# GpSimd's scoring work queued behind the first candidates, in a decoder trunk with product-key experts

## The chip, the cores and the metric

The kernel runs on one core of a Trainium2 chip. Its time is the device time of one execution in microseconds; the number that counts is the median of the runs. The core has five engines with their own instruction queues: TensorE (PE, with its weight loads as PEld), VectorE (DVE), ScalarE (ACT), GpSimd (POOL) and SyncE (SP, which here only issues DMAs). Each queue is worked off in order. An instruction waits at the head of its queue until what it needs has been signalled, and all behind it wait too.

## The reference

A batch of one sequence of 512 tokens of 1024 features goes through two layers. Layer 0 mixes along the sequence with a gated linear recurrence, layer 1 with multi-head latent attention. Each mixer is preceded by an RMSNorm whose shift, scale and gate come from a conditioning vector, and each is followed by the same channel mixer, which is the larger part of the work:

```python
def peer(h, w_q, sub_keys, u_tab, v_tab):
    q = (h @ w_q).reshape(B, S, PEER_HEADS, 2, PEER_HALF)
    s = jnp.einsum('bshpd,hpnd->bshpn', q, sub_keys)
    v1, i1 = lax.top_k(s[..., 0, :], 16); v2, i2 = lax.top_k(s[..., 1, :], 16)
    cand = v1[..., :, None] + v2[..., None, :]          # 256 sums per head
    cv, ci = lax.top_k(cand.reshape(..., 256), 16)      # best 16 pairs
    idx = e1 * 128 + e2                                 # one expert of 16384
    g = softmax(cv)
    act = gelu(einsum('bcd,bchkd->bchk', h, u_tab[idx]))
    out = einsum('bchk,bchkd->bcd', g * act, v_tab[idx])
```

The modulation vectors are `silu(c) @ ada_w + ada_b`: 112 columns of 128 values, each the sum over a row of 1024 products ("ada" below).

## The kernel before, in words

Tokens are four blocks of 128; features lie on partitions as eight chunks `k`. Products that need float32 precision are made of three matmuls: each operand is split into a high part (ACT copies it into the matmul's format, L179, `whi`) and a low part (source minus high part, L180, `wlo`, on an engine that the caller names), and `mm3` (L216 to L218) adds low times high, high times low and high times high. A weight or expert tile takes a DMA into `raw` (four buffers), one ACT instruction and one subtraction.

Each layer ends in `peer(l)`. Three of the four token blocks are computed densely: for each of 128 expert tiles, `u_part` splits the tile of `u` and multiplies it with the activations of 384 tokens (24 matmuls of 128x384), ACT applies the gelu, and later the tile of `v` is multiplied with the gated result. The fourth block (number 3, `nd`) gathers the rows of its own experts by indirect DMA on GpSimd's queue and reduces them on DVE (`gather_steps`, L1479 to L1488, named `grow` and `gdot`). The stages are:

1. The head. The last products of the mixer (`wo`) come out in two halves of 256 tokens. For each half, DVE adds the residual (L383), ACT squares it (L287), and the squares are summed in `nacc`: three additions on GpSimd (chunks 1 to 3) and three on DVE (chunks 4 to 6), L288 in `half_sq`. PE sums `nacc` over the partitions (L297, outputs `wo` or `st`), ACT and DVE make the reciprocal root, PE turns it into a row, ACT copies it (L310). Then for each chunk DVE makes `xn` (L1091), ACT the high part of `h` (L1093), DVE the low part (L1094), and PE multiplies three tiles of the query weights with it as soon as a chunk is there (`pq`, L216 to L218).
2. Scoring, four groups of two heads. A group multiplies four tiles of query weights (`pq`, 96 matmuls of 128x512), scores the keys (`sc`, L1200), and DVE takes the top 16 for each of the four token blocks (L933 to L937). GpSimd adds the candidates (`cand`, two instructions for each block: L944 and L947), DVE takes the best pairs (L956 to L960). In the same stretch each group does `UPQ` = 3 expert tiles, and `adas_pool` makes 6 ada columns in layer 0 or 2 in layer 1. A column there is a load on SP's queue (two buffers), a multiplication on GpSimd (L168), a sum on ACT (L169); a column is closed by a small addition on GpSimd (L174). In this stretch all splits of weights and expert tiles after the first three `pq` tiles have their subtraction on GpSimd.
3. Decoding, on DVE, of block 3 first (its indices start the gathers) and then of block 0. `UDEC` expert tiles are written ahead of it.
4. Gates: for each 16 tokens of the three dense blocks, DVE makes two pairs of one-hot tiles (`oo` L1041, `pr` L1043), PE multiplies them (`wps`, 32 matmuls), ACT copies them out (L1052), and expert tiles go on in between.
5. The rest: `v` tiles (`acc`) with the remaining gathers.

The order on each engine is made when the program is built: a scheduler simulates the engines and takes what is ready first, by the order in the code. `tc.issue_after(ins)` is a constraint on it: what the block traces on the engine of `ins` is queued behind `ins`. It adds no wait on a semaphore, and it does not bind the other engines. `self.hold` does the same for the first splits against the last steps of the head on ACT and DVE.

Lines to know: `half_sq` L270 to L289, `adas_pool` L161 to L175, `wtile` L184 to L199, `candidates` L939 to L949, the scoring loop L1182 to L1211, `UDEC` at L47 and its use at L1216.

Of the kernel before, what the change touches and what calls it, by code (L numbers as in the profile page):

```python
# [16 lines left out]
OP = mybir.AluOpType  # L17
# [4 lines left out]
P = 128  # L22
D = 1024
KC = D // P
# [19 lines left out]
OWN = KC * T // ND  # L44
LEAD = OWN + RING - 3 + SPILL
UPQ = (3, 3, 3, 3)
UDEC = 13  # L47
UEND = 7
QUIET = 4
EARLY = 74  # L50
# [33 lines left out]
class Trunk:  # L84
# [854 lines left out]
    def candidates(self, pool, v, h0, n):  # L939
        nc = self.nc  # L940
        v4 = v.rearrange("p (h s) k -> p h s k", s=2)[:, h0:h0 + n]
        cand = pool.tile([P, n, NCAND], F32, name="cand", bufs=3)
        ca = cand[:, :, 0:64].rearrange("p h (i j) -> p h i j", j=16)
        nc.gpsimd.tensor_tensor(ca, v4[:, :, 0, 0:4].unsqueeze(3).to_broadcast([P, n, 4, 16]),  # L944
                                v4[:, :, 1, 0:16].unsqueeze(2).to_broadcast([P, n, 4, 16]), op=OP.add)
        cb = cand[:, :, 64:112].rearrange("p h (i j) -> p h i j", j=4)
        nc.gpsimd.tensor_tensor(cb, v4[:, :, 0, 4:16].unsqueeze(3).to_broadcast([P, n, 12, 4]),  # L947
                                v4[:, :, 1, 0:4].unsqueeze(2).to_broadcast([P, n, 12, 4]), op=OP.add)
        return cand  # L949

    def best_pairs(self, pool, cand, cv, ci, h0, n):
# [105 lines left out]
    def peer(self, l):  # L1057
        nc, io, tc = self.nc, self.io, self.tc
        nd = NB - 1
        with ExitStack() as st:  # L1060
# [6 lines left out]
            h = []  # L1067
# [54 lines left out]
            def ring(t):  # L1122
                held = (t - OWN) % RING < RING - 3
                return acts.tile([P, ND], F32, name="gact" if held else "gsp", bufs=RING - 3 if held else 3)
# [3 lines left out]
            def u_part(after=None, eng=None):  # L1128
                t = state["u"]
                state["u"] = t + 1  # L1130
                out = self.bank("u", True)
                hi, lo = self.wtile(io["uT"][l][t], KC, eng=eng or nc.vector)
                with tc.issue_after(after) if after is not None else ExitStack():
                    for k, (bh, bl) in enumerate(h):
                        self.mm3(out[:, :ND], (hi[:, k, :], lo[:, k, :]), (bh[:, :ND], bl[:, :ND]), k == 0, k == KC - 1)
                if t < OWN:
                    gact[t] = self.x.rearrange("p k t -> p (k t)")[:, t * ND:t * ND + ND]
                elif LEAD - SPILL <= t < LEAD:
                    g = acts.tile([P, ND], F32, name="gsp", bufs=3)
                    nc.scalar.activation(g, out[:, :ND], AF.Gelu)  # L1140
                    nc.scalar.dma_start(self.gscr[l, t - (LEAD - SPILL)], g)
                    return
                else:
                    gact[t] = ring(t)
                nc.scalar.activation(gact[t], out[:, :ND], AF.Gelu)
# [13 lines left out]
            def decodes(bs):  # L1159
                for b in bs:  # L1160
                    res = []
                    for _ in self.decode(dpool, cvs[b], cis[b], iu[b], res):
                        yield
                    if b == nd:
                        gsel.append(self.gather_index(gpool, l, *res))
                    else:
                        prep[b] = self.gate_prep(pool, *res)

            with tc.tile_pool(name=f"pq{l}", bufs=1) as pool:
                waiting = []  # L1170

                def settle(keep):
                    nonlocal gsteps
                    while len(waiting) > keep:
                        b, grp, cand = waiting.pop(0)
                        self.best_pairs(pool, cand, cvs[b], cis[b], 2 * grp, 2)
                        if grp == 3 and b == nd:
                            for _ in decodes((nd,)):
                                pass
                            gsteps = self.gather_steps(gpool, l, *gsel[0], hn)  # L1180

                for grp in range(4):  # L1182
                    keys = pool.tile([P, 4, P], F32, name="keys", bufs=2)
                    nc.scalar.dma_start(keys, io["keysT"][l][:, 4 * grp:4 * grp + 4, :])
                    outs = []
                    wq = l * 16 + 4 * grp
                    if grp == 0:
                        outs = pq0
                    qs = []
                    for m in range(4):  # L1190
                        if m >= len(outs):
                            outs.append(self.bank("pq"))
                            self.lin(outs[m], self.wtile(io["w_pq"][wq + m], KC, eng=nc.gpsimd), h)
                        q = pool.tile([P, T], F32, name="pq_s", bufs=5)
                        nc.scalar.activation(q, outs[m], AF.Copy)
                        qs.append(q)
                    for b in (nd, *range(nd)):
                        sc = self.bank("sc")
                        for m in range(4):
                            nc.tensor.matmul(sc[:, m * P:m * P + P], qs[m][:, b * P:b * P + P], keys[:, m, :],  # L1200
                                             start=True, stop=True)
                        for m in range(4):
                            last = self.topk_half(pool, sc[:, m * P:m * P + P], vs[b][:, 4 * grp + m, :],
                                                  iu[b][:, 4 * grp + m, :])
                        waiting.append((b, grp, self.candidates(pool, vs[b], 2 * grp, 2)))
                        settle(1)
                    self.hold = ()
                    self.adas_pool(6 if l == 0 else 2, pool)
                    for _ in range(UPQ[grp]):
                        u_part(eng=nc.gpsimd)  # L1210
                settle(0)  # L1211
            with tc.tile_pool(name=f"gate{l}", bufs=1) as pool:
                nsg = P // TG
                steps = decodes(range(nd))
                for i in range(UDEC):
                    u_part()  # L1216
# [5 lines left out]
                for i in range(nt):  # L1222
# [3 lines left out]
                    w, p = self.gate_group(pool, l, i // nsg, i % nsg, *prep[i // nsg])  # L1226
# [13 lines left out]
            grp, vls, vdma = {}, [], []  # L1240
# [110 lines left out]
            outs = [hpool.tile([P, D], F32, name=f"onat{b}", tag=f"h{b}") for b in range(nd)] + [next(gsteps)]  # L1351
# [232 lines left out]
```

## Time and profile before

| | us |
|---|---|
| median of 3 runs | 2978.91 |
| lowest and highest of these | 2976.91, 2980.32 |
| the profiled execution, its own time | 2977.65 |
| its span, first to last instruction | 2975.9 |
| PE busy | 2879.1 (97%) |
| DVE busy | 2500.0 (84%) |
| POOL busy | 1115.1 (37%) |

The profile's rows give start, duration, engine, line, operation, output and inputs; a bracket tells the idle time of the engine ahead of the instruction and what ended it. In a table of groups a row has the count, the busy time in us and the mean in ns. In the table of waits a row reads: engine, its instruction, what it waited for, us in total, how often, the longest. Matmuls overlap, so the time that one costs is the step from its start to the next one's, which is shorter than the duration in its row. PEclk is the granted clock of TensorE as a share of full speed.

### The profile page before, as it was taken

The page shows a single profiled execution, that of the slowest core. Times are in us where ns is not written, and L with a number is a line of the kernel's source. Part 1 is how long each engine was busy: PE and PEld are TensorE (multiplying, and loading weights), DVE is VectorE, ACT ScalarE, POOL GpSimd, SP SyncE. Part 2 cuts the span into 40 slices and gives each one's busy share as a digit, 9 for nine tenths or more (in the row PEclk, how much of TensorE's full clock was granted, in tenths as well). Part 3 has the DMA queues.
Part 4 walks back from the last instruction along what each step waited for, and adds up shares of the span by engine and source line. Part 5 has one row for each costly group of instructions (what it writes and reads, how often), then busy time and mean ns, then how long its engine had stood idle before and what let it go on. Part 6 is the DMA issues. An engine that isn't in the chain of part 4 may idle for free.

```text
span 2975.9 us, 43994 instructions
## 1 busy us (share of the span) xinstructions
PE 2879.1 (97%) x15680; PEld 2570.0 (86%) x15680; DVE 2500.0 (84%) x4709; ACT 1423.6 (48%) x2103; POOL 1115.1 (37%) x873
## 2 busy tenths in 40 slices
PE   7979998999999999999999989989999999999998
PEld 5679998999888889998878789989998888899997
DVE  8988799998888878879878877899985777788888
ACT  4755355665433333333576752456664333333333
POOL 4038514432222234535334455235331111244442
PEclk9989999999999999999999989999999999999999
DMA  8546349998999999999323333379999899999996
GB/s 317 186 156 198 115 158 345 360 370 325 338 361 360 361 320 356 320 346 326 107 85 130 123 138 103 114 276 346 371 355 315 300 336 323 309 329 353 347 337 220
DMA packets 296219, 813.71 MB, mean 273 GB/s; under 512 B 33152, under 2 KB 130560, under 8 KB 289600
## 3 DMA queue, kind: packets, MB, share of 16 engines
q1 hardware_dynamic: 188928, 439.41, 42.9%
q0 software_dynamic: 78912, 287.34, 27.0%
q10 hardware_dynamic: 28160, 84.14, 7.3%
q8 instruction: 124, 2.03, 0.3%
q14 instruction: 95, 0.78, 0.1%
HBM read 727.44 MB, written 83.36 MB: 272 GB/s over the span
## 4 chain that ended last, share of the span: by engine, by line
PE 86%; DVE 6%; ACT 3%; DMA 2%; issue 2%; POOL 1%; SPq 0%; ACTq 0%; DVEq 0%; POOLq 0%
PE acc L217 12%; PE acc L218 12%; PE acc L216 12%; PE u L216 12%; PE u L218 11%; PE u L217 11%; PE pq L217 2%; PE pq L218 2%; PE pq L216 2%; PE wps L1049 1%; PE wps L208 1%; PE sc L1200 1%; DVE wlo L180 1%; ACT whi L179 1%; DVE ada_junk L153 1%
## 5 line engine op out<-in xcount | busy, mean ns | idle before, releaser
L216 PE MATMUL u<-h,wlo 128*128 128x384 f32 x2048 | 692.3, 338 | 10.7 <-ACT gsp L1140 10.4
L218 PE MATMUL u<-h,whi 128*128 128x384 f32 x2048 | 689.3, 337 | 0.0
L217 PE MATMUL u<-h,whi 128*128 128x384 f32 x2048 | 687.8, 336 | 0.0
L1479 POOL DMA_INDIRECT grow<-in_u_dram,idx x256 | 340.5, 1330 | 714.2 <-DVE gdot L1483 449.7
L218 PE MATMUL acc<-vh,ah 128*128 128x512 f32 x1512 | 589.4, 390 | 0.0
L217 PE MATMUL acc<-vl,ah 128*128 128x512 f32 x1512 | 589.1, 390 | 0.0
L1479 POOL DMA_INDIRECT grow<-in_v_dram,idx x256 | 375.1, 1465 | 564.8 <-DVE gacc L1488 381.9
L216 PE MATMUL acc<-vh,al 128*128 128x512 f32 x1512 | 549.0, 389 | 1.1 <-ACT vh L179 1.1
L179 ACT ACTIVATE whi<-raw 128x1024 fp32r<-128x1024 f32 (+2 forms) x362 | 352.8, 976 | 176.0 <-PE u L218 67.1
L180 DVE TENSOR_TENSOR vl<-vraw,vh 128x1024 fp32r<-128x1024 f32 x252 | 308.6, 1225 | 122.7 <-ACT vh L179 121.5
L216 PEld LDWEIGHTS u<-h,wlo 128*128 128x128 f32 x2048 | 386.1, 189 | 16.3 <-ACT gsp L1140 13.3
L217 PEld LDWEIGHTS u<-h,whi 128*128 128x128 f32 x2048 | 385.9, 188 | 2.8
L218 PEld LDWEIGHTS u<-h,whi 128*128 128x128 f32 x2048 | 385.6, 188 | 0.0
L180 DVE TENSOR_TENSOR wlo<-raw,whi 128x1024 fp32r<-128x1024 f32 (+1 forms) x263 | 322.1, 1225 | 75.2 <-ACT whi L179 74.6
L218 PEld LDWEIGHTS acc<-vh,ah 128*128 128x128 f32 x1512 | 283.7, 188 | 59.2
L216 PEld LDWEIGHTS acc<-vh,al 128*128 128x128 f32 x1512 | 283.7, 188 | 58.4 <-ACT vh L179 1.5
L217 PEld LDWEIGHTS acc<-vl,ah 128*128 128x128 f32 x1512 | 283.8, 188 | 57.4
L1488 DVE SCALAR_TENSOR_TENSOR gacc<-grow,gdot,gacc 128x1024 f32<-128x1024 f32 x254 | 324.9, 1279 | 7.9 <-DMA grow<-in_v_dram,idx 6.8
L1483 DVE CUSTOM_DVE_ANT_0 grow<-grow,hn 128x1024 f32<-128x1024 f32 x256 | 308.5, 1218 | 13.8 <-DMA grow<-in_u_dram,idx 13.5
L179 ACT ACTIVATE ah<-gact 128x384 fp32r<-128x384 f32 x204 | 106.8, 523 | 425.5 <-PE acc L218 327.5
L179 ACT ACTIVATE vh<-vraw 128x1024 fp32r<-128x1024 f32 x252 | 264.2, 1048 | 57.8 <-issue 45.0
L1052 ACT ACTIVATE stg<-wps 128x512 f32<-128x512 f32 x192 | 188.8, 1113 | 58.2 <-PE wps L208 58.1
(421 smaller groups left out, 4595.9 us busy)
## 6 DMA issues: line engine op xcount, KB each, us to landing
raw<-in_uT_dram SPq DMA_DIRECT2D x256, 512.0 KB, 6.0
vraw<-in_v_dram SPq DMA_DIRECT2D x256, 512.0 KB, 6.2
wscr<-stg ACTq DMA_DIRECT2D x48, 1024.0 KB, 7.3
wt<-wscr SPq DMA_DIRECT2D x42, 1024.0 KB, 10.5
ada_raw<-in_adaw_dram SPq DMA_DIRECT2D x76, 512.0 KB, 4.3
gscr<-gsp ACTq DMA_DIRECT2D x132, 192.0 KB, 6.1
gact<-gscr SPq DMA_DIRECT2D x108, 192.0 KB, 6.4
ada_raw<-in_adaw_dram POOLq DMA_DIRECT2D x36, 512.0 KB, 6.2
```

The lines of the kernel that those rows point to most:

```text
L153: nc.vector.tensor_tensor_reduce(junk, raw, self.csil, op0=OP.mult, op1=OP.add, scale=1.0, scalar=b, accum_out=col)
L179: last = nc.scalar.activation(hi, src, AF.Copy)
L180: lo = (eng or nc.vector).tensor_tensor(lo, src, hi.bitcast(F32), op=OP.subtract)
L208: return pe.add_instruction(mybir.InstMatmult(name=self.nc.get_next_instruction_name(), start_tensor_calc=start, stop_tensor_calc=stop, ld ...
L216: nc.tensor.matmul(out, al, bh, start=first, stop=False, **kw)
L217: nc.tensor.matmul(out, ah, bl, start=False, stop=False, **kw)
L218: last = nc.tensor.matmul(out, ah, bh, start=False, stop=last, **kw)
L1049: lead = nc.tensor.matmul(out, w, pr[:, 0, a + t], start=True, stop=False).ins
L1052: nc.scalar.activation(stg[:, :, c:c + 4].rearrange("p e t -> p t e"), wps.rearrange("p (t e) -> p t e", t=4), AF.Copy, scale=1.0 / GSCALE)
L1479: nc.gpsimd.indirect_dma_start(out=row, out_offset=None, in_=tabs[s], in_offset=bass.IndirectOffsetOnAxis(ap=idx[:, k:k + 1], axis=0))
L1483: nc.vector.tensor_tensor_reduce(row, row, hn, op0=OP.mult, op1=OP.add, scale=1.0, scalar=0.0, accum_out=col)
L1488: nc.vector.scalar_tensor_tensor(acc, row, col, acc, op0=OP.mult, op1=OP.add)
```

## The change

Three edits. The second instruction of the first group's first candidates (those of block 3) becomes a mark, `first`. Ada columns, and from the second group on the splits of weight tiles, are queued behind that mark on GpSimd; the expert tiles are too. In the first group, the subtractions of the one weight tile and the three expert tiles go to DVE instead of GpSimd. And `UDEC` goes from 13 to 15.

```diff
-UDEC = 13
+UDEC = 15
...
     def candidates(self, pool, v, h0, n):
...
-        nc.gpsimd.tensor_tensor(cb, ...)
+        self.last_cand = nc.gpsimd.tensor_tensor(cb, ...).ins
...
-                waiting = []
+                waiting, first = [], None
...
                         if m >= len(outs):
                             outs.append(self.bank("pq"))
-                            self.lin(outs[m], self.wtile(io["w_pq"][wq + m], KC, eng=nc.gpsimd), h)
+                            with tc.issue_after(first) if first is not None else ExitStack():
+                                w = self.wtile(io["w_pq"][wq + m], KC, eng=nc.gpsimd if grp else nc.vector)
+                            self.lin(outs[m], w, h)
...
                         waiting.append((b, grp, self.candidates(pool, vs[b], 2 * grp, 2)))
+                        first = first or self.last_cand
                         settle(1)
                     self.hold = ()
-                    self.adas_pool(6 if l == 0 else 2, pool)
-                    for _ in range(UPQ[grp]):
-                        u_part(eng=nc.gpsimd)
+                    with tc.issue_after(first):
+                        self.adas_pool(6 if l == 0 else 2, pool)
+                        for _ in range(UPQ[grp]):
+                            u_part(eng=nc.gpsimd if grp else nc.vector)
```

From the scoring loop on, line numbers of the changed kernel are 1 to 4 higher (L1195 becomes L1197, L1483 becomes L1487).

The order of the queues shows what this moves. First GpSimd's queue in layer 0, from the additions of the head on; `nacc` is the sum of squares, `ada_raw` an ada column. Before:

```order
L288 TENSOR_TENSOR nacc_1459<-nacc_1459,sq_1469 128x256
L168 TENSOR_TENSOR ada_raw_2148<-ada_raw_2148,csil_66 128x1024
L288 TENSOR_TENSOR nacc_1459<-nacc_1459,sq_1479 128x256
L168 TENSOR_TENSOR ada_raw_2152<-ada_raw_2152,csil_66 128x1024
L288 TENSOR_TENSOR nacc_1459<-nacc_1459,sq_1489 128x256
L168 TENSOR_TENSOR ada_raw_2156<-ada_raw_2156,csil_66 128x1024
L288 TENSOR_TENSOR nacc_1459<-nacc_1459,sq_1545 128x256
L168 TENSOR_TENSOR ada_raw_2160<-ada_raw_2160,csil_66 128x1024
L288 TENSOR_TENSOR nacc_1459<-nacc_1459,sq_1555 128x256
L288 TENSOR_TENSOR nacc_1459<-nacc_1459,sq_1565 128x256
L168 TENSOR_TENSOR ada_raw_2164<-ada_raw_2164,csil_66 128x1024
L168 TENSOR_TENSOR ada_raw_2168<-ada_raw_2168,csil_66 128x1024
```

The same place in the changed kernel, where `cand_2013` are the first candidates (`v3` is block 3), `wlo_2274` is the first split of the second group, and `cand_2045` are the candidates of block 0:

```order
L288 TENSOR_TENSOR nacc_1459<-nacc_1459,sq_1469 128x256
L288 TENSOR_TENSOR nacc_1459<-nacc_1459,sq_1479 128x256
L288 TENSOR_TENSOR nacc_1459<-nacc_1459,sq_1489 128x256
L288 TENSOR_TENSOR nacc_1459<-nacc_1459,sq_1545 128x256
L288 TENSOR_TENSOR nacc_1459<-nacc_1459,sq_1555 128x256
L288 TENSOR_TENSOR nacc_1459<-nacc_1459,sq_1565 128x256
L947 TENSOR_TENSOR cand_2013<-v3_1924 128x2x48
L168 TENSOR_TENSOR ada_raw_2148<-ada_raw_2148,csil_66 128x1024
L168 TENSOR_TENSOR ada_raw_2152<-ada_raw_2152,csil_66 128x1024
L944 TENSOR_TENSOR cand_2013<-v3_1924 128x2x64
L180 TENSOR_TENSOR wlo_2274<-raw_2272,whi_2273 128x1024
L947 TENSOR_TENSOR cand_2045<-v0_1921 128x2x48
```

The six additions now stand together, with nothing between them and the first candidates. Before, thirteen ada multiplications and five splits stood between the first addition and the first candidates in layer 0, and eight and five in layer 1; now none do. Of the five splits, four are on DVE and one is behind the candidates.

Second, DVE's queue in layer 0 at chunks 3 to 7 of the head's second half (`xn` L1091 and `h` L1094; `h4_1722` is chunk 4), up to the first MAX of the scoring. Before:

```order
L1094 SCALAR_TENSOR_TENSOR h3_1705<-xn_1827,mod_91,h3_1705 128x256
L1091 SCALAR_TENSOR_TENSOR xn_1861<-x_68,gs_f0_1628,nacc_1459 128x256
L1094 SCALAR_TENSOR_TENSOR h4_1722<-xn_1845,mod_91,h4_1722 128x256
L1091 SCALAR_TENSOR_TENSOR xn_1877<-x_68,gs_f0_1628,nacc_1459 128x256
L1094 SCALAR_TENSOR_TENSOR h5_1736<-xn_1861,mod_91,h5_1736 128x256
L1091 SCALAR_TENSOR_TENSOR xn_1893<-x_68,gs_f0_1628,nacc_1459 128x256
L1094 SCALAR_TENSOR_TENSOR h6_1750<-xn_1877,mod_91,h6_1750 128x256
L1094 SCALAR_TENSOR_TENSOR h7_1764<-xn_1893,mod_91,h7_1764 128x256
```

And in the changed kernel, with the splits that came from GpSimd (`wlo_1954` is the fourth `pq` tile, the other three are the expert tiles of the first group):

```order
L1094 SCALAR_TENSOR_TENSOR h3_1705<-xn_1827,mod_91,h3_1705 128x256
L1091 SCALAR_TENSOR_TENSOR xn_1861<-x_68,gs_f0_1628,nacc_1459 128x256
L180 TENSOR_TENSOR wlo_1954<-raw_1952,whi_1953 128x1024
L180 TENSOR_TENSOR wlo_2176<-raw_2174,whi_2175 128x1024
L1094 SCALAR_TENSOR_TENSOR h4_1722<-xn_1845,mod_91,h4_1722 128x256
L1091 SCALAR_TENSOR_TENSOR xn_1877<-x_68,gs_f0_1628,nacc_1459 128x256
L1094 SCALAR_TENSOR_TENSOR h5_1736<-xn_1861,mod_91,h5_1736 128x256
L1091 SCALAR_TENSOR_TENSOR xn_1893<-x_68,gs_f0_1628,nacc_1459 128x256
L1094 SCALAR_TENSOR_TENSOR h6_1750<-xn_1877,mod_91,h6_1750 128x256
L1094 SCALAR_TENSOR_TENSOR h7_1764<-xn_1893,mod_91,h7_1764 128x256
L180 TENSOR_TENSOR wlo_2208<-raw_2206,whi_2207 128x1024
L180 TENSOR_TENSOR wlo_2240<-raw_2238,whi_2239 128x1024
```

Two splits now stand ahead of chunk 4, and two behind chunk 7, ahead of the first MAX.

Third, DVE's queue in layer 0 at the second group of gates: `pr` is what PE's `wps` waits for; `grow` with `gdot` is one gathered row block, which waits for its indirect DMA (`grow_4462` and `grow_4496` are the sixth, `grow_4465` and `grow_4499` the seventh). Before:

```order
L1483 ISA grow_4462,gdot_4284<-grow_4462,hn_1627 128x1024
L1483 ISA gdot_4284 128x1
L1043 TENSOR_TENSOR pr_4399<-oo_4398,gp_4143 128x2048
L1483 ISA grow_4465,gdot_4284<-grow_4465,hn_1627 128x1024
L1483 ISA gdot_4284 128x1
L180 TENSOR_TENSOR wlo_4645<-raw_4643,whi_4644 128x1024
L1043 TENSOR_TENSOR pr_4423<-oo_4422,gp_4143 128x2048
```

And in the changed kernel:

```order
L1487 ISA grow_4496,gdot_4352<-grow_4496,hn_1627 128x1024
L1487 ISA gdot_4352 128x1
L1487 ISA grow_4499,gdot_4352<-grow_4499,hn_1627 128x1024
L1487 ISA gdot_4352 128x1
L1043 TENSOR_TENSOR pr_4433<-oo_4432,gp_4209 128x2048
L180 TENSOR_TENSOR wlo_4573<-raw_4571,whi_4572 128x1024
L1043 TENSOR_TENSOR pr_4457<-oo_4456,gp_4209 128x2048
```

The seventh block stood behind the third `pr` and ahead of the fourth, and is now ahead of both. The number of splits that DVE does ahead of the first `pr` is 19 in both. On PE, between the scoring and the first `wps` stand 508 matmuls of `u` instead of 502, and between the first 32 `wps` and the next ones, which wait for the third `pr`, 66 matmuls of `u` instead of 48.

More of the change, by code (lines that the diff above doesn't have):

```diff
@@ L946, in candidates @@
         cb = cand[:, :, 64:112].rearrange("p h (i j) -> p h i j", j=4)
-        nc.gpsimd.tensor_tensor(cb, v4[:, :, 0, 4:16].unsqueeze(3).to_broadcast([P, n, 12, 4]),
-                                v4[:, :, 1, 0:4].unsqueeze(2).to_broadcast([P, n, 12, 4]), op=OP.add)
+        self.last_cand = nc.gpsimd.tensor_tensor(cb, v4[:, :, 0, 4:16].unsqueeze(3).to_broadcast([P, n, 12, 4]),
+                                v4[:, :, 1, 0:4].unsqueeze(2).to_broadcast([P, n, 12, 4]), op=OP.add).ins
         return cand
```

## The prediction

> **What bounds the kernel now.** I read the page first, then PE's waits by stage, then the windows, and the timelines of the two heads.
>
> ```profile
> span 2975.9 us, 43994 instructions
> PE 2879.1 (97%) x15680; PEld 2570.0 (86%) x15680; DVE 2500.0 (84%) x4709; ACT 1423.6 (48%) x2103; POOL 1115.1 (37%) x873
> ```
>
> PE is the bound: it idles 2975.9 − 2879.1 = 96.8 us of the whole span, so a change that takes no work off PE can only win idle time and time at a low clock. The change touches the two heads and what follows them. PE's waits there, first in layer 0 (178 to 240 us):
>
> ```profile
> PE wo L297 <- DVE nacc L288: 6.5, 1, 6.5
> PE pq L217 <- DVE h L1094: 5.9, 4, 2.5
> PE pq L216 <- ACT h L1093: 4.9, 1, 4.9
> ```
>
> In layer 1 (1700 to 1765 us):
>
> ```profile
> PE st L297 <- DVE nacc L288: 5.3, 1, 5.3
> PE pq L217 <- DVE h L1094: 5.3, 4, 2.6
> ```
>
> At the start of the gates in layer 0:
>
> ```profile
> PE wps L1049 <- DVE pr L1043: 8.1, 2, 5.5
> ```
>
> The windows give the same four places with the granted clock (busy us of PE, PEld, DVE, ACT, POOL, then PEclk, DMA share, GB/s):
>
> ```profile
> 181.80:239.70 57.90, 40.50 (x236) 38.31 (x236) 35.96 (x47) 31.73 (x67) 35.48 (x20) 0.76 0.47 166
> 1710.50:1761.50 51.00, 40.14 (x232) 37.33 (x232) 38.92 (x47) 29.49 (x62) 30.21 (x19) 0.80 0.40 145
> 451.00:471.00 20.00, 11.94 (x75) 11.54 (x74) 16.98 (x26) 7.62 (x9) 8.49 (x6) 0.74 0.98 367
> 1973.00:1993.00 20.00, 12.11 (x76) 11.71 (x75) 17.15 (x26) 7.34 (x9) 8.90 (x7) 0.74 0.99 376
> ```
>
> Layer 0's head idles 57.90 − 40.50 = 17.4 us, and what is busy runs at 0.76: at most 40.50 × 0.24 = 9.7 us more. Layer 1's idles 10.9 us and loses at most 40.14 × 0.20 = 8.0 us. The timeline of layer 0's head shows the clock in the steps between matmuls:
>
> ```profile
> 203.28 0.58 PE L217 MATMUL pq<-h,whi 128*128 128x256 f32 x1 [2.49 <-DVE h L1094]
> 211.34 0.28 PE L216 MATMUL pq<-h,xlo 128*128 128x256 f32 x1
> 211.46 0.28 PE L217 MATMUL pq<-h,xhi 128*128 128x256 f32 x1
> 218.27 0.58 PE L217 MATMUL pq<-h,whi 128*128 128x256 f32 x1 [1.57 <-DVE h L1094]
> 218.65 0.41 PE L218 MATMUL pq<-h,whi 128*128 128x256 f32 x1
> 218.86 0.41 PE L216 MATMUL pq<-h,xlo 128*128 128x256 f32 x1
> ```
>
> Behind a wait the step is 0.21 us (218.65 to 218.86), later 0.12 (211.34 to 211.46). From 203.28 to 211.34 PE did 31 products and eight small sums in 8.06 us, worth about 4.6 at the quick step (31 × 0.12, and the sums by half): 3.5 us lost in this stretch, and a second one begins at 218.27. I count 7 us in each head: 17.4 + 7 = 24.4 us lost in layer 0 and 10.9 + 7 = 17.9 us in layer 1. The gate starts lose 8.1 and 20.00 − 12.11 = 7.9 us of waiting, and 11.94 × 0.26 = 3.1 us each of clock.
>
> **The heads, what goes.** The timeline of the sums in layer 0:
>
> ```profile
> 178.73 0.74 POOL L288 TENSOR_TENSOR nacc<-nacc,sq 128x256 f32<-128x256 f32 x1 [11.64 <-ACT sq L287]
> 180.77 2.37 POOL L168 TENSOR_TENSOR ada_raw<-ada_raw,csil 128x1024 f32<-128x1024 f32 x1 [1.30 <-DMA ada_raw<-in_adaw_dram]
> 181.89 0.48 DVE L383 SCALAR_TENSOR_TENSOR x<-wo,mod,x 128x256 f32<-128x256 f32 x1 [0.17 <-PE wo L218]
> 186.84 1.48 DVE L288 TENSOR_TENSOR nacc<-nacc,sq 128x256 f32<-128x256 f32 x3 [4.47 <-POOL nacc L288]
> 188.38 1.01 PE L297 MATMUL wo<-ones,nacc 128*128 128x1 f32 x4 [6.53 <-DVE nacc L288]
> ```
>
> An ada multiplication of 2.37 us stands behind an addition of 0.74 us, and by the order of the queue another ahead of the third addition; DVE then waits 4.47 us and PE 6.53. PE came at 188.38 − 6.53 = 181.85. Without the multiplications GpSimd ends its three additions by 178.73 + 3 × 0.74 = 181.0, if the squares are there; DVE's three, at 0.49 each, can follow its residual of 181.89 or stand ahead of it, so they end at about 183.4 and PE waits **1.5 us** (0 to 2). In layer 1 GpSimd's additions have no ada ahead of them either; there I take **0** (0 to 1.5).
>
> Second, DVE's own chunk work is slower whenever GpSimd works:
>
> ```profile
> 222.05 4.74 POOL L180 TENSOR_TENSOR wlo<-raw,whi 128x1024 fp32r<-128x1024 f32 x2 [4.52 <-ACT whi L179]
> 224.40 2.67 DVE L1094 SCALAR_TENSOR_TENSOR h<-xn,mod,h 128x256 fp32r<-128x256 f32 x1 [2.63 <-ACT h L1093]
> 227.39 0.47 DVE L1094 SCALAR_TENSOR_TENSOR h<-xn,mod,h 128x256 fp32r<-128x256 f32 x1
> ```
>
> The same instruction takes 2.67 us beside GpSimd's split and 0.47 behind it. With GpSimd empty from the last addition to the first candidates, the waits for `h` (5.9 + 4.9 us, and 5.3) go, but for the first one. Sum, row, `xn` and `h` of chunk 0 are a chain that PE may not hide wholly. Its least is 0, its most the 2.49 us of the row at 203.28; I take **1.4 us** in each layer, about the middle.
>
> What is put in their place: DVE gets four splits. With no work on GpSimd beside it, one takes 1.21 us, and two lie behind chunk 7, in a gap, so that they cost nothing:
>
> ```profile
> 204.34 1.21 DVE L180 TENSOR_TENSOR xlo<-raw,xhi 128x1024 fp32r<-128x1024 f32 x1
> 239.69 0.49 PE L1200 MATMUL sc<-keys,pq_s 128*128 128x128 f32 x3
> 243.04 0.52 DVE L933 MAX8 v<-sc 128x8 f32<-128x128 f32 x2 [9.68 <-PE sc L1200]
> ```
>
> If that cover of 9.68 us were gone they would delay the first MAX by 2.4 us, and the first candidates with it. The other two stand in the chain ahead of chunk 4: **2 us** taken (0 if PE has chunks in hand, 2.4 if not).
>
> Third, the clock. A wait of only 1.57 us was enough for a slow stretch, and some waits remain: I leave **one stretch of 3.5 us** in each head (0 to 7). The Trainium skill (TensorE: Matmul & The Clock Gate, "Why this matters for your kernels") puts the drop at idle gaps over about 3 us; the row at 218.27 speaks against it, and the rival below has what it would give.
>
> **Scoring, what moves.** All ada columns and the second group's first splits now queue behind the first candidates. GpSimd's prices there (243 to 360 us), and PE's group:
>
> ```profile
> L180 POOL TENSOR_TENSOR wlo<-raw,whi 128x1024 fp32r<-128x1024 f32 x22 | 52.7, 2403 | 8.2 <-ACT whi L179 7.4 <-POOL mod L174 0.8
> L168 POOL TENSOR_TENSOR ada_raw<-ada_raw,csil 128x1024 f32<-128x1024 f32 x13 | 31.4, 2417 | 0.2 <-DMA ada_raw<-in_adaw_dram 0.2
> L944 POOL TENSOR_TENSOR cand<-v 128x128 f32<-128x128 f32 x12 | 5.0, 415 | 4.4 <-DVE v L936 4.4
> ```
>
> ```profile
> 253.15 0.33 PE L218 MATMUL u<-h,whi 128*128 128x384 f32 x1
> 253.33 0.39 PE L216 MATMUL pq<-h,wlo 128*128 128x512 f32 x1
> ```
>
> The later rows are of the chain of waits (the start of the third group's `pq`, and that group's scores) and of the timeline:
>
> ```profile
> 291.37 0.23 PE pq L216
> ```
>
> ```profile
> 313.18 2.68 PE sc L1200 x24
> ```
>
> ```profile
> 321.55 0.35 POOL L947 TENSOR_TENSOR cand<-v 128x96 f32<-128x96 f32 x1 [4.30 <-DVE v L936]
> ```
>
> A group of layer 0 asks GpSimd for 7 splits, 6 ada columns and 8 candidates: 7 × 2.403 + 6 × 2.417 + 8 × 0.415 = 34.6 us. PE's group takes 291.37 − 253.33 = 38.0 us. So GpSimd keeps up with 3.4 us to spare per group, but starts with nothing in hand. Only the first `pq` tile of the second group is late: where GpSimd waits for DVE, as at 321.55, the candidates come 321.55 − 313.18 = 8.4 us behind the scores. From there stand 0.42 + 2 × 2.42 + 0.42 + 2.40 = 8.1 us in the queue (candidates, two ada, candidates, split), so the split ends 16.5 us behind the scores. PE wants it 253.33 − 239.69 = 13.6 us behind them, plus five more `u` matmuls at 0.18: 14.5. PE waits **2.0 us** (0 to 5). The ada loads on SP's queue share two buffers; in the changed order the raw loads of this group stand ahead of those that wait, and the loads of the next ones have a group's time, so I cost that at nothing; without the slack it is what the backlog rival prices. ACT's ada sums come along; ACT is 48% busy. In layer 1 there are 2 columns a group, 9.7 us less, and I take no wait.
>
> **The gates.** By the order, 18 more matmuls of `u` stand between the first `wps` and the next, and 6 more ahead of the first: PE comes 24 × 0.18 = 4.3 us later at the third `pr`. DVE, though, has the seventh gathered block ahead of it now:
>
> ```profile
> 455.17 0.22 PE L1049 MATMUL wps<-pr,oo 128*128 128x128 f16 x1 [2.58 <-DVE pr L1043]
> 458.14 1.23 DVE L1483 CUSTOM_DVE_ANT_0 grow<-grow,hn 128x1024 f32<-128x1024 f32 x1 [3.02 <-DMA grow<-in_u_dram,idx]
> 460.43 1.22 DVE L1043 TENSOR_TENSOR pr<-oo,gp 128x2048 f16<-128x2048 f16 x1
> ```
>
> With a `pr` of 1.22 us behind it, the third one ends at 458.14 + 1.23 + 1.22 = 460.6. PE came for it at 455.17 − 2.58 = 452.6 and now comes at 456.9; the waits of 2.6 and 5.5 us become one of 3.7 us, and the fourth `pr` is there when PE has done the next 24 matmuls of `u`. So **4.4 us** less per layer, with −2 (the DMA later still) and 11 (wait and low clock both gone) as ends. What these matmuls do at their old place is the same work; the stage's total hardly changes.
>
> **The sum.** Layer 0's head: 24.4 − (1.5 + 1.4 + 2 + 3.5 + 2.0) = 14.0 saved. Layer 1's: 17.9 − (0 + 1.4 + 2 + 3.5) = 11.0. Gates 2 × 4.4 = 8.8. Together 33.8. The profiled execution took 2977.65 us, with 1.75 outside its span, and lies 1.3 below the median of 2978.91; 2977.65 − 33.8 = 2943.9, which on the scale of the median is 2945.1.
>
> **Rivals.** *The low clock goes whole.* By the 3 us rule no wait that I leave is long enough, both slow stretches go, and 33.8 + 7 = 40.8 are saved: 2938.1 us. Against it the rows at 218.27 to 218.86; for it that the waits of 6.5, 5.3 and 4.9 us are the ones that vanish. 0.12.
>
> *Half a head.* Another chain in the head (squares on ACT, the row, the two splits ahead of chunk 4, a raw load that comes late) takes the place of GpSimd, and the gates give nothing: 25.0 / 2 = 12.5, 2966 us, with 10 to 25 as ends: 2954 to 2969. For it: PE's waits name ACT and DVE as often as GpSimd. 0.23.
>
> *GpSimd's backlog starves PE* in layer 0's scoring. Group after group PE would wait for splits behind ada columns. GpSimd's mean over 13 large instructions is 2.41 us; PE waits from (38.0 − 3.3) / 13 = 2.67 us on. It takes the 33.8 us back when three groups lose 11.3 us each, at a mean of 3.54 us. A load held up behind an ada column waiting on its buffer would do it too. Then 2981 us or more. Against it: the rows above, where GpSimd works beside DVE's MAX at 2.4 us. 0.07.
>
> *Nothing changes*: the first candidates' mark holds no work back, or the gains and the new waits cancel, about 2979. 0.08.
>
> **How the numbers follow.** My forecast, 2945.1 us, has 0.50. Its own ends: 2932 (gates whole, 2 × 6.6 more) to 2958 (−2 instead of 4.4 at each gate). The range of 2930 to 2966 takes in the clock rival and most of the half head. A difference under 0.2%, 6 us, can't be told from none: the forecast, the clock and the half head (0.85) lie beyond it on the quick side, 0.08 within, 0.07 slower.
>
> **What would show it.** PE's wait at the sums under 2 us; `h` at 0.47 us throughout both heads; the granted clock of the heads over 0.9; the first `pq` of the second group waiting about 2 us for GpSimd; one wait of about 4 us at the gates. Wrong, if PE waits for `wlo` of GpSimd group after group, or the head's idle time stays over 10 us.

## The result and the profile after

The changed kernel takes 2934.66 us in the median (2926.37 to 2935.77), before 2978.32 us; the ratio is 0.9847 (95% interval 0.9828 to 0.9866). 2945.1 was forecast: right in direction and within the range, 10 us too cautious. The page of the changed kernel, whose profiled execution took 2935.30 us:

```profile
span 2933.5 us, 43947 instructions
PE 2868.5 (98%) x15680; PEld 2561.6 (87%) x15680; DVE 2469.5 (84%) x4717; ACT 1424.2 (49%) x2103; POOL 1104.4 (38%) x865
```

The span is 42.4 us shorter: PE idles 65.0 instead of 96.8 us, and the same 15680 matmuls keep it busy for 10.6 us less, at a granted clock of 0.993 instead of 0.985. PE's waits in the head of layer 0, then of layer 1, each up to the first scores:

```profile
PE wo L297 <- DVE nacc L288: 1.7, 1, 1.7
PE pq L216 <- ACT h L1093: 0.9, 1, 0.9
PE pq L217 <- DVE h L1094: 0.6, 1, 0.6
```

```profile
PE pq L216 <- ACT h L1093: 0.9, 1, 0.9
PE st L297 <- DVE nacc L288: 0.7, 1, 0.7
PE pq L217 <- DVE h L1094: 0.6, 1, 0.6
```

Of 17.3 us of waiting in layer 0's head 3.2 are left, and of 10.9 in layer 1's 2.2. The first `pq` of the second group waits 0.6 us for GpSimd's split, in either layer. The windows of the four places, from PE's arrival at the sums to the first scores, and 20 us of each gate start (columns as before):

```profile
183.75:222.50 38.75, 35.50 (x231) 34.05 (x231) 24.21 (x51) 22.16 (x47) 3.25 (x3) 0.87 0.36 131
1687.90:1724.20 36.30, 34.03 (x230) 32.56 (x231) 22.95 (x48) 21.34 (x46) 2.97 (x3) 0.91 0.35 122
438.10:458.10 20.00, 17.80 (x115) 17.26 (x115) 17.50 (x23) 9.97 (x13) 8.75 (x6) 0.91 1.00 390
1937.90:1957.90 20.00, 15.80 (x104) 15.26 (x103) 15.51 (x22) 9.29 (x11) 7.72 (x5) 0.91 0.93 338
```

GpSimd is nearly empty in both heads now, with 3.25 and 2.97 us of work, the last additions. The stretches that took 57.90 and 51.00 us take 38.75 and 36.30. For the stage times I use the starts of the scores, first the row of layer 0 before, then both after:

```profile
L1200 PE MATMUL sc<-keys,pq_s x128: 270/275/275, 239.7 to 354.7; 128*128 128x128 f32 x128
```

```profile
L1202 PE MATMUL sc<-keys,pq_s x128: 271/275/275, 222.5 to 339.2; 128*128 128x128 f32 x128
L1202 PE MATMUL sc<-keys,pq_s x128: 271/275/275, 1724.2 to 1841.0; 128*128 128x128 f32 x128
```

Measured between landmarks of PE, layer 0's head gives 19.1 us back (from the mixer's `ri`, which began 1.9 us later in this execution, to the first scores), layer 1's 15.0 (from `lat`). From the first scores to the first `wps` it is 4.3 and 2.3 us longer: 11 and 8 matmuls of `u` more keep PE busy for 2.7 and 1.7 us there, and it waits for 1.6 and 0.6 us (0.6 for the split; 1.0 for ACT's `gact` in layer 0). The gates with what follows them are 9.6 and 7.2 us shorter. −1.9 + 19.1 − 4.3 + 9.6 + 15.0 − 2.3 + 7.2 = 42.4.

### The profile page after: what moved, and what is told of

It is laid out like the page before. It is cut to its first block, busy times and chain, and to the rows that moved or that the text cites. A ratio compares the mean times of both kernels' runs of the same rounds, so it can differ in the third digit from the quotient of the medians.

```text
span 2933.5 us, 43947 instructions
## 1 busy us (share of the span) xinstructions
PE 2868.5 (98%) x15680; PEld 2561.6 (87%) x15680; DVE 2469.5 (84%) x4717; ACT 1424.2 (49%) x2103; POOL 1104.4 (38%) x865
## 4 chain that ended last, share of the span: by engine, by line
PE 85%; DVE 8%; ACT 3%; issue 2%; DMA 1%; POOL 1%; ACTq 0%; SPq 0%; DVEq 0%; POOLq 0%
PE acc L218 12%; PE acc L217 12%; PE acc L216 12%; PE u L216 11%; PE u L217 10%; PE u L218 10%; PE pq L216 2%; PE pq L217 2%; PE pq L218 2%; DVE wlo L180 2%; PE wps L1049 1%; PE wps L208 1%; PE sc L1202 1%; PE pv L849 1%; DVE ada_junk L153 1%
## 5 line engine op out<-in xcount | busy, mean ns | idle before, releaser
L1483 POOL DMA_INDIRECT grow<-in_u_dram,idx x256 | 355.1, 1387 | 712.2 <-DVE gdot L1487 455.8
L1483 POOL DMA_INDIRECT grow<-in_v_dram,idx x256 | 373.5, 1459 | 546.3 <-DVE gacc L1492 357.4
L180 DVE TENSOR_TENSOR wlo<-raw,whi 128x1024 fp32r<-128x1024 f32 x271 | 334.9, 1237 | 88.5 <-ACT whi L179 88.3
L1487 DVE CUSTOM_DVE_ANT_0 grow<-grow,hn 128x1024 f32<-128x1024 f32 x256 | 309.4, 1219 | 17.0 <-DMA grow<-in_u_dram,idx 17.0
```

Of the source, the lines that this page charges most:

```text
L180: lo = (eng or nc.vector).tensor_tensor(lo, src, hi.bitcast(F32), op=OP.subtract)
L1483: nc.gpsimd.indirect_dma_start(out=row, out_offset=None, in_=tabs[s], in_offset=bass.IndirectOffsetOnAxis(ap=idx[:, k:k + 1], axis=0))
L1487: nc.vector.tensor_tensor_reduce(row, row, hn, op0=OP.mult, op1=OP.add, scale=1.0, scalar=0.0, accum_out=col)
```

## The experiments

The theory: the ada columns in the heads, between the additions and beside DVE's chunk work, are most of the gain; `UDEC` is the rest; the splits on DVE only replace those on GpSimd. Rivals: the two tiles of `UDEC` carry it; the splits do; or the low clock does. Medians in us; "before" is that of the same set of runs. The changed kernel's own ratio was 0.9847 (0.9828 to 0.9866), so those of runs 1, 5 and 6 overlap with it, and what they differ by has to be read from the traces too.

| run | median | before | ratio (95%) |
|---|---|---|---|
| 1 changed, UDEC 13 | 2939.13 | 2978.16 | 0.9865 (0.9848 to 0.9881) |
| 2 before, UDEC 15 | 2964.25 | 2978.16 | 0.9952 (0.9936 to 0.9969) |
| 3 ada columns only | 2938.31 | 2978.16 | 0.9866 (0.9849 to 0.9882) |
| 4 splits on DVE only | 2971.78 | 2978.16 | 0.9979 (0.9969 to 0.9988) |
| 5 changed, clock covered | 2927.97 | 2977.30 | 0.9835 (0.9822 to 0.9849) |
| 6 ada columns, UDEC 15 | 2931.74 | 2977.30 | 0.9853 (0.9839 to 0.9866) |
| 7 ada behind the additions | 2944.23 | 2977.30 | 0.9892 (0.9877 to 0.9907) |
| 8 changed, UDEC 17 | 2944.34 | 2977.30 | 0.9896 (0.9881 to 0.9911) |
| 9 ada between the additions | 2947.17 | 2978.26 | 0.9900 (0.9885 to 0.9915) |
| 10 before, clock covered | 2986.79 | 2978.26 | 1.0028 (1.0017 to 1.0038) |
| 11 run 6, clock covered | 2924.84 | 2978.26 | 0.9826 (0.9813 to 0.9840) |

**Runs 1 and 2: UDEC.**

```diff
# run 1, against the changed kernel
-UDEC = 15
+UDEC = 13
# run 2, against the kernel before
-UDEC = 13
+UDEC = 15
```

> The changed kernel with UDEC back at 13; everything ahead of the gates as in the changed kernel. If the heads carry most of the gain: the first scores stay within 2 us of the changed kernel's 222.5 and 1724.2 us, PE waits about 8 us for pr in each layer again instead of 4.4 and 4.0, the gate window loses its clock again, and the time is 7 to 12 us above the changed kernel, 2942 to 2947 us. If the two tiles carry most of it: 2955 us or more.

> The kernel before with UDEC at 15 and nothing else. If the heads carry most of the gain: the heads idle as before (sums wait 6.5 and 5.3 us), only the gates get shorter, 7 to 12 us below before, 2966 to 2971 us. If the two tiles carry most of it: under 2955 us. If the parts help each other only: within 3 us of before.

Run 1 is 4.5 us above the changed kernel, less than expected; run 2 is 13.9 us below before, somewhat more. In run 2 the heads (from `ri` and `lat` to the first scores) take 154.1 and 311.5 us, before 154.0 and 309.6; in run 1 they take 132.3 and 296.3 us, in the changed kernel 134.9 and 294.6. The first scores of layer 0 come at 217.9 us in run 1, 4.6 earlier than in the changed kernel and not within the 2 us expected: `ri` began 2.0 us earlier, and the head has one slow stretch of the clock less (the last section has it). PE's waits at the gates' start in run 1, layer 0 and layer 1:

```profile
PE wps L1049 <- DVE pr L1043: 7.2, 2, 4.7
PE wps L1049 <- DVE pr L1043: 7.0, 2, 4.4
```

So the two tiles shorten the gates and not the heads, by 13.9 us alone and by 4.5 on top of the rest; the heads carry the rest.

**Run 3: the ada columns only.**

```diff
+                        first = first or self.last_cand
                         settle(1)
...
-                    self.adas_pool(6 if l == 0 else 2, pool)
+                    with tc.issue_after(first):
+                        self.adas_pool(6 if l == 0 else 2, pool)
```

> The kernel before with the ada columns queued behind the first candidates and nothing else; the four splits stay on GpSimd ahead of the candidates, behind the six additions. If the ada multiplications between and beside the additions are the cause: the waits at the sums fall to about 2 and 1 us as in the changed kernel, the two splits beside the second half's chunks still stretch an L1094 or L1091 to over 2 us at two to four places, and the time falls by 20 to 28 us. If DVE's chunk work is slow beside any large instruction of GpSimd and that costs most: 8 to 15 us.

It gives 39.9 us, more than expected: nearly all of the change. The two splits beside the second half did stretch the chunk work, as the timeline of GpSimd and DVE in layer 0 shows:

```profile
204.64 4.93 POOL L180 TENSOR_TENSOR wlo<-raw,whi 128x1024 fp32r<-128x1024 f32 x2 [17.28 <-ACT whi L179]
...
205.95 1.38 DVE L1094 SCALAR_TENSOR_TENSOR h<-xn,mod,h 128x256 fp32r<-128x256 f32 x1 [1.59 <-ACT h L1093]
207.25 2.61 DVE L1091 SCALAR_TENSOR_TENSOR xn<-x,gs_f,nacc 128x256 f32<-128x256 f32 x1
```

But PE did not wait for it. Its waits in that head are these:

```profile
PE wo L297 <- DVE nacc L288: 2.6, 1, 2.6
PE pq L217 <- DVE h L1094: 0.6, 1, 0.6
PE pq L216 <- ACT h L1093: 0.5, 1, 0.5
```

That is a step that I had wrong: in the second half DVE is ahead of PE by then, so a stretch there, or two splits in the chain, makes PE wait for nothing.

**Run 4: the splits only.**

```diff
-                            self.lin(outs[m], self.wtile(io["w_pq"][wq + m], KC, eng=nc.gpsimd), h)
+                            self.lin(outs[m], self.wtile(io["w_pq"][wq + m], KC, eng=nc.gpsimd if grp else nc.vector), h)
...
-                        u_part(eng=nc.gpsimd)
+                        u_part(eng=nc.gpsimd if grp else nc.vector)
```

> The kernel before with the first group's four splits on DVE and nothing else; the ada multiplications stay between the additions and beside the chunks. If the ada columns are the cause: the waits at the sums stay at 6.5 and 5.3 us, chunk work still shows instructions of over 2 us, and the time is within 8 us of before, on either side. If the splits on GpSimd are the cause: 15 us or more below before.

6.4 us below before, within what was expected. The head keeps its waits (layer 0), and the one at the sums grows from 6.5 to 8.7 us:

```profile
PE wo L297 <- DVE nacc L288: 8.7, 1, 8.7
PE pq L217 <- DVE h L1094: 5.1, 3, 2.7
PE pq L216 <- ACT h L1093: 2.6, 1, 2.6
```

Where the 6.4 us lie was not settled: layer 0's head is no shorter, layer 1's by 2.3 us, and the gates with what follows by 4.1 and 3.6 us, with the tiles in another order.

**Run 6: the ada columns and UDEC 15, no split moved** (run 3 with `UDEC = 15`).

> The changed kernel without the four splits on DVE and without holding back the weight and expert tiles: before with the ada columns behind the first candidates and UDEC at 15. If the splits on DVE bring nothing, since DVE is ahead of PE in the second half of the head: within 3 us of the changed kernel, on either side. If GpSimd's splits beside the last chunks, or the missing five splits ahead of the candidates, matter: 4 to 8 us above it.

2931.74 us: 2.9 below the changed kernel, with intervals that overlap. On top of the other two edits, the splits on DVE and the holding back of weight and expert tiles bring nothing that can be measured here. It is the smaller change with the same time. Alone the three edits give 39.9, 13.9 and 6.4 us, together 43.7: the parts don't add up. Each also changes the order of what follows, which may be why; no run separates that.

**Runs 7 and 9: order or neighbours.** Both put a few ada columns back into the heads, behind the additions (7) or between them (9).

```diff
# run 7 (last_add is GpSimd's last addition of the head)
-                    with tc.issue_after(first):
+                    with tc.issue_after(first if grp else self.last_add):
                         self.adas_pool(6 if l == 0 else 2, pool)
# run 9
+                    n = 6 if l == 0 else 2
+                    if grp == 0:
+                        self.adas_pool(min(n, 4), pool)
+                        n -= min(n, 4)
                     with tc.issue_after(first):
-                        self.adas_pool(6 if l == 0 else 2, pool)
+                        self.adas_pool(n, pool)
```

> The changed kernel with the first group's ada columns (six in layer 0, two in layer 1) queued behind the last addition of the head instead of behind the first candidates: nothing stands between the additions, but large GpSimd work stands beside the chunk work again. If most of the loss was the order between the additions and the clock behind their wait: the sums still wait 1.7 us and the time is within 4 us of the changed kernel. If the stretch of DVE's chunk work beside GpSimd was most of it: PE waits 3 us or more for h again, with L1091 or L1094 at over 2 us there, and the time is 6 to 12 us above it.

> The changed kernel with the first four ada columns (two in layer 1) free on GpSimd again: in layer 0 they then stand between the six additions, all others stay behind the first candidates and nothing of GpSimd's large work stands beside the second half's chunks. If the order between the additions is what costs: the sums wait 5 to 7 us again in layer 0 (1.7 in the changed kernel), DVE's additions wait for GpSimd's, and the time is 8 to 16 us above the changed kernel. If it was mostly the stretch beside the chunks: the sums wait 2 to 4 us and the time is 2 to 7 us above it.

Run 7 is 9.6 us above the changed kernel, run 9 12.5. In run 9 the sums wait again, in layer 0 and in layer 1:

```profile
PE wo L297 <- DVE nacc L288: 8.7, 1, 8.7
PE st L297 <- DVE nacc L288: 5.2, 1, 5.2
```

But run 9 is not the order alone. DVE's three additions ahead of these sums, first in layer 0 and then in layer 1:

```profile
188.79 3.65 DVE L288 TENSOR_TENSOR nacc<-nacc,sq 128x256 f32<-128x256 f32 x3 [4.48 <-POOL nacc L288]
1695.26 4.29 DVE L288 TENSOR_TENSOR nacc<-nacc,sq 128x256 f32<-128x256 f32 x3 [0.38 <-POOL nacc L288]
```

At 0.41 us each they would take about 1.2 us. In layer 0 the 4.48 us of waiting for GpSimd's addition are the order, and 3.65 − 1.2 = 2.4 us are a stretch beside the next column; together they are the 7.0 us by which the wait grew (1.7 to 8.7). In layer 1 the stretch is 3.1 of the 4.5 us (0.7 to 5.2). So both mechanisms are real; run 7 has the stretch alone, and run 9 has both.

In run 7 the sums do not wait longer than in the changed kernel, but the first chunk does. Layer 1, where only two columns came back (GpSimd, DVE, ACT, PE):

```profile
1696.41 4.84 POOL L168 TENSOR_TENSOR ada_raw<-ada_raw,csil 128x1024 f32<-128x1024 f32 x2
...
1691.82 0.41 DVE L288 TENSOR_TENSOR nacc<-nacc,sq 128x256 f32<-128x256 f32 x1
...
1696.58 2.48 DVE L288 TENSOR_TENSOR nacc<-nacc,sq 128x256 f32<-128x256 f32 x1
1698.98 0.47 DVE L385 SCALAR_TENSOR_TENSOR x<-wo,mod,x 128x256 f32<-128x256 f32 x1
1699.37 2.17 DVE L288 TENSOR_TENSOR nacc<-nacc,sq 128x256 f32<-128x256 f32 x1
1701.46 0.87 DVE L1093 SCALAR_TENSOR_TENSOR xn<-x,gs_f,nacc 128x256 f32<-128x256 f32 x2
...
1701.97 0.51 ACT L1095 ACTIVATE h<-xn,mod 128x256 fp32r<-128x256 f32 x1 [2.01 <-DVE xn L1093]
...
1702.53 0.58 PE L216 MATMUL pq<-h,wlo 128*128 128x256 f32 x1 [4.75 <-ACT h L1095]
```

Two multiplications, 4.84 us together, turn two of DVE's additions from 0.41 into 2.48 and 2.17 us. They stand ahead of the first `xn` in DVE's queue, and PE's wait there grows from 0.9 to 4.75 us: the 3.8 us of the stretch, one for one. The row is named by ACT's `h`; the cause is two steps back, on an engine that the row does not name. ACT's sums of the columns moved along with the multiplications, but they are not what holds this `h` up: ACT idles 2.01 us ahead of it, for DVE's `xn`. The residual of L383 (here L385), with one input from PSUM, stays at 0.47 us.

**Run 8: more of UDEC** (`UDEC = 17`).

> The changed kernel with two more expert tiles ahead of the gates, UDEC at 17. If the gates still wait for the gathered rows that DVE needs ahead of the third pr, PE arrives 8.3 us later and the waits of 4.4 and 4.0 us go: 3 to 9 us below the changed kernel. If the added tiles only move work that is then missing later: within 2 us.

9.7 us above the changed kernel, where a gain or nothing was expected. PE came later at the third `pr`, but the `pr` came later still: all waits for `pr` together are 7.1 us in each layer, 4.4 and 4.0 in the changed kernel. The row of that wait, and the gathered block on DVE ahead of the `pr`, in run 8:

```profile
449.90 0.27 PE L1049 MATMUL wps<-pr,oo 128*128 128x128 f16 x1 [3.83 <-DVE pr L1043]
...
447.48 1.23 DVE L1487 CUSTOM_DVE_ANT_0 grow<-grow,hn 128x1024 f32<-128x1024 f32 x1 [4.42 <-DMA grow<-in_u_dram,idx]
```

In the changed kernel:

```profile
445.16 0.22 PE L1049 MATMUL wps<-pr,oo 128*128 128x128 f16 x1 [2.04 <-DVE pr L1043]
...
442.74 1.23 DVE L1487 CUSTOM_DVE_ANT_0 grow<-grow,hn 128x1024 f32<-128x1024 f32 x1 [2.50 <-DMA grow<-in_u_dram,idx]
...
428.27 1.22 DVE L1487 CUSTOM_DVE_ANT_0 grow<-grow,hn 128x1024 f32<-128x1024 f32 x1
...
429.77 1.67 POOL L1483 DMA_INDIRECT grow<-in_u_dram,idx  x1 [26.21 <-DVE gdot L1487]
```

The seventh gathered block is used 442.74 − 222.5 = 220.2 us behind the first scores there, and 447.48 − 218.9 = 228.6 us in run 8. The last two rows tell why. The gathered blocks share four buffers (`GROWS`), so the fifth gather (429.77) waits on GpSimd until DVE's first product (428.27) has freed one. DVE does 22 splits between the first scores and that product in run 8, 20 in the changed kernel, so the product starts 211.9 instead of 205.8 us behind the first scores, and the fifth gather, 1.5 us behind it in both, comes later with it. That is 6.1 of the 8.4 us. Of the three values of `UDEC` that were run, 13, 15 and 17, 15 is the best; its neighbours were not run.

**Runs 5, 10 and 11: the clock.** Matmuls that feed nothing fill PE's idle time in the heads (the numbers in run 5; the others change the kernel they start from, or the counts).

```diff
+    def cover(self, bank, n):
+        e = self.iota_e.rearrange("p n e -> p (n e)")
+        for _ in range(n):
+            with self.tc.issue_after(self.tail):
+                self.tail = self.nc.tensor.matmul(bank[:, :T // 2], e[:, :P], e[:, :T // 2], start=True, stop=True).ins
...
-                    col = self.half_sums(outs[0], 0)
+                    col = self.half_sums(outs[0], 0, 14)
...
+                        if (i, k) == (0, 0):
+                            self.cover(sums, 8)
```

> The changed kernel with idle time of PE in the heads filled by matmuls that feed nothing: ahead of the first half's sums 14 (layer 0) and 6 (layer 1) of 128x256, ahead of the first chunk 8 in each layer; they add no result. If short waits (1.75, and 0.91 with 0.59) are what drops the clock: the granted clock stays at 0.97 or more in both heads, no step of 0.21 us follows, and the time is 4 to 9 us below the changed kernel. If the clock falls in the heads for another reason, or only behind gaps over 3 us: the heads keep a stretch at 0.5 and the time is within 2 us of the changed kernel, or up to 2 above.

> The kernel before with matmuls that feed nothing in the idle time of its heads: 54 and 44 of 128x256 ahead of the first half's sums, 40 in layer 0 and 2 in layer 1 ahead of the first chunk; they add no result. The ada columns stay where they were. If about 7 us a head was the low clock: the granted clock of the heads goes from 0.76 and 0.80 to over 0.93, DVE's waits stay, and the time is 6 to 13 us below before. If the clock is not what the waits cost: within 3 us of before, or above it.

> The two parts that seem to carry the gain, and the cover: before with the ada columns behind the first candidates, UDEC at 15, and 14 and 6 idle matmuls ahead of the first half's sums and 8 ahead of the first chunk (they add no result); no split moved to DVE. If the splits on DVE bring nothing and the clock falls behind short waits: 2921 to 2928 us, 3 to 8 below the same kernel without the cover (2931.7) and at or below the changed kernel with it (2928.0). If GpSimd's splits matter once the clock is whole: over 2929 us.

Run 5 is 6.7 us below the changed kernel, as expected. Two windows of layer 0's head in the changed kernel, then in run 5:

```profile
186.50:190.00 3.50, 3.50 (x19) 3.50 (x18) 1.85 (x5) 0.93 (x3) 1.79 (x2) 0.52 0.43 150
194.00:200.00 6.00, 6.00 (x30) 6.00 (x29) 4.61 (x11) 2.35 (x6) 0.00 (x0) 0.50 0.94 337
```

```profile
186.50:190.00 3.50, 3.50 (x32) 3.40 (x32) 2.91 (x9) 1.82 (x6) 1.67 (x2) 1.00 0.51 154
194.00:200.00 6.00, 5.94 (x49) 5.78 (x49) 5.57 (x16) 4.01 (x10) 0.00 (x0) 1.00 0.75 262
```

Behind the wait of 1.75 us, and again behind 0.91 and 0.59, PE worked at half its clock, 19 matmuls in 3.5 us; with the idle time filled it does 32, though the eight one-column sums behind the first wait are still there. Run 11 adds the cover to run 6 and is the fastest kernel here, 2924.84 us, 6.9 below run 6. How much of this is the clock of the heads is less sure. Between the profiled executions, run 5's heads are 4.1 and 1.7 us shorter than the changed kernel's, of 9.8 us in all. Run 11's are 129.4 and 292.4 us, run 6's 131.8 and 291.9: 1.9 us less, of 11.6, and most of the rest lies behind the first `wps`. So the cover keeps the clock up, and two pairs of kernels gain about 7 us with it, but not all of that was found in the heads.

Run 10 went against its expectation: the kernel before, with its long waits filled, is 8.5 us slower. The cover did not do there what it was meant to: from PE's arrival to the first scores the clock rose from 0.76 and 0.80 to 0.86 and 0.82, where over 0.93 was expected. In layer 0 the clock rose, from 0.91 to 0.95 between `ri` and the first scores, but that stretch took 155.6 instead of 154.0 us: PE still waited for DVE and ACT. In layer 1 it is 10.6 us longer, 4.6 of them ahead of the sums, with waits for ACT's `h` of 5.4 us where there were 0.3. The scheduler also put one ada column more ahead of the splits on GpSimd, and made other shifts of that kind, so this run does not test the clock alone, and its 8.5 us are not explained in full. That a faster PE only waits longer while a chain of other engines sets the end, so that the clock I counted as a loss of the kernel before was partly hidden behind the chain, is a guess that fits; it is not shown.

## Why the prediction was right, point by point

**The bound and the cause** held. GpSimd's ada columns stretched and interrupted the heads' chain; run 3 shows them alone to be 39.9 us.

**What remains in the heads** was close: 1.5 against 1.75 us at the sums of layer 0, 0 against 0.75 in layer 1, 1.4 against 0.9 + 0.6 at the first chunk, in both. The 1.4 was the middle of a wide range, so that it fits is luck in part. Two terms were off and canceled in layer 0: the two splits ahead of chunk 4 cost 0 and not 2 us (run 3 shows why), and the slow clock cost more than one stretch of 3.5 us. By the windows above it is up to 35.50 × 0.13 = 4.6 us in layer 0 and 34.03 × 0.09 = 3.1 in layer 1, and the sign of a clock over 0.9 did not come in layer 0 (0.87). The whole head of layer 0, from `ri` on:

```profile
87.60:222.50 134.90, 131.65 (x631) 104.33 (x630) 112.83 (x182) 91.25 (x146) 11.81 (x18) 0.96 0.47 161
```

**What the heads had lost before** was the term that was too small. I counted 17.4 us idle and 7 of clock in layer 0, from the sums on. The head gave 19.1 us back, 0.9 of it five matmuls that moved: 18.2. With 3.2 + 4.6 = 7.8 us still lost, it had lost about 26.0, not 24.4. The bound of 9.7 us beside my count leaves room for that: I had counted two slow stretches and left out a third, 17 steps of 0.21 us from 190.5 to 194.1 us, behind the wait of 6.53 us. (In the first stretch the trace has 29 products where I wrote 31; its loss is then 3.7 us instead of 3.5.) Layer 1's head gave 15.0 us back, 0.4 of it two matmuls, where 11.0 were forecast. There too nothing was lost at the splits (2 us taken), and the count of 7 us of clock was the same guess, with a bound of 8.0. Together the heads gave 34.1 us where 14.0 + 2.0 + 11.0 = 27.0 were forecast (the 2.0 is the late `pq` of scoring, which stood in layer 0's sum). The row of before, from `ri` on:

```profile
85.70:239.70 154.00, 136.60 (x636) 108.61 (x635) 126.06 (x181) 100.35 (x165) 44.12 (x34) 0.91 0.49 174
```

**Scoring** held. GpSimd keeps up, no wait comes back group after group; the late first `pq` waits 0.6 instead of 2.0 us, and the same in layer 1, where I took none. The 1.0 us for ACT's `gact` in layer 0 I had not seen coming. The mark did hold the work back.

**The gates** were under-counted: 4.4 us each by the wait for `pr`, and 9.6 and 7.2 us measured, one us of that by fewer matmuls. As the stretch ahead of them grew by 4.3 and 2.3 us, the two stages together gave 5.3 and 4.9 us, 10.2 where 2 × 4.4 − 2.0 = 6.8 were forecast. The waits for `pr` add up about as forecast (3.7; measured 4.4 and 4.0), but in layer 0 not as the one wait at the third `pr`: that is 2.0 us, and three shorter ones come later. The missing part is what I left out of the sum: the low clock at the gates' start, 0.74 before and 0.91 now, which shows in 1.7 and 0.4 us less busy time besides the moved matmuls, and PE's waits for ACT's `gsp` further on, 5.2 and 5.2 us before, 1.5 and 4.4 now.

**The rivals.** No backlog; not half a head. PE's rows of waits in the heads name only DVE and ACT; GpSimd stands a step further back, and run 3 shows that it was the cause. The clock rival gave a better number, 2938.1, by a wrong reason: slow stretches did not vanish, they are there behind waits of 1.75 us and less. The Trainium skill (TensorE: Matmul & The Clock Gate, "Why this matters for your kernels") names idle gaps over about 3 us; the traces disagree, and in run 5, with all but one wait of 0.59 us filled or nearly so, the slow stretches are gone.

## What to carry to other kernels

Work on an engine that is 37% busy is not free: ask what it stands between in its own queue, and whose instructions it slows while it runs. With six or fewer columns a layer put back, the second alone cost 10 us here, and both together 12.5. Look at the short waits too, once the long ones are gone: 36 idle matmuls kept the clock up, and two kernels came out about 7 us faster with them. And take the parts of a change singly, alone and on top of the others: of three edits, one carries 40 of 44 us, and one adds nothing measurable to the other two.

## What the runs showed of the hardware that I had not expected

The clock falls behind short waits, and not each time. Run 1 has the same head as the changed kernel, with waits of 1.76, 0.91 and 0.59 us. These are its windows behind the first and around the other two:

```profile
185.00:190.00 5.00, 4.31 (x26) 4.11 (x25) 2.99 (x10) 2.08 (x6) 1.34 (x2) 0.74 0.32 105
190.00:194.00 4.00, 3.12 (x22) 2.72 (x22) 4.00 (x10) 3.00 (x7) 0.00 (x0) 1.00 0.78 328
```

One slow stretch here, two in the changed kernel: its head is 132.3 us from `ri` to the first scores, the changed kernel's 134.9, and they differ by one matmul at most. Five of the kernels wait 2.6 us at most at any place of their heads (the changed one and runs 1, 3, 6 and 8). In layer 0 each has at least one slow stretch; in layer 1, behind waits of 0.75, 0.93 and 0.59 us, only the changed kernel and run 1 do. Run 6 there, with these waits unfilled, from PE's arrival at the sums to the first scores:

```profile
1687.40:1719.30 31.90, 29.57 (x220) 28.02 (x221) 22.32 (x45) 20.16 (x44) 10.31 (x6) 1.00 0.37 133
```

In the four covered heads of runs 5 and 11 there is none. The Trainium skill (same page, "Part 1: The HAM clock gate") says that the window it watches runs freely and the phase differs from run to run; that fits these rows, which do not show the window itself.

DVE's additions with both inputs in SBUF wait out a GpSimd instruction beside them, 0.41 against 2.48 us in run 7. It goes the other way too: in the changed kernel two of GpSimd's additions take 2.61 us beside a split on DVE, where one alone takes 0.72.

```profile
184.44 0.72 POOL L288 TENSOR_TENSOR nacc<-nacc,sq 128x256 f32<-128x256 f32 x1 [1.44 <-ACT sq L287]
185.76 2.61 POOL L288 TENSOR_TENSOR nacc<-nacc,sq 128x256 f32<-128x256 f32 x2 [0.59 <-ACT sq L287]
...
185.76 1.21 DVE L180 TENSOR_TENSOR xlo<-raw,xhi 128x1024 fp32r<-128x1024 f32 x1
```

The Trainium skill (SBUF — State Buffer, "Who interferes with whom") says so of DVE with two inputs and a GpSimd that reads; the trace agrees.
